# The convolution's channel norm placed behind the fifth half pair of w_out, and two sets of buffers for the latent attention

## The chip, the cores and the metric

One Trainium2 chip, of which the kernel uses 1 core. The metric is the time of one execution on the device in microseconds; the kernel before has a median of 2216.26 us over three runs. TensorE is called PE here, VectorE DVE, ScalarE ACT, GpSimd POOL and SyncE SP, as the profile calls them.

## What is computed

Two blocks in float32 on a sequence of 256 tokens of width 2048. The first has two layers, each a convolution branch and a window attention, joined by `w_out`; the second is one layer of RWKV-7 and latent attention (MLA) side by side, and a feed-forward network. Cut to what the change touches:

```python
def first_block(...):                       # for each of two layers
    u = rmsnorm(h) @ w_in
    a_val, a_glu, a_z, q, k, v, b_z = split(u)
    y  = conv31(a_val * sigmoid(a_glu)) + conv_b
    yc = y - mean(y, channels)              # the channel norm
    y  = yc * rsqrt(mean(yc * yc) + EPS) * cln_g + cln_b
    ya = silu(y) * silu(a_z)
    yb = window_attention(q, k, v) * silu(b_z)
    h  = h + concat([ya, yb]) @ w_out
    h  = h + rmsnorm(p @ w_pe) * sigmoid(h @ w_pg)
...
def mla_mixer(...):                         # 8 heads, taken in 4 pairs
    q = rms_norm(c_q) @ w_uq;  kv = rms_norm(c_kv) @ w_ukv
    s = q_nope . k_nope + rope(q_pe) . rope(k_pe)
    out = softmax(causal(s)) @ v
...
x = x + concat([y_rwkv, y_mla]) @ w_out_2
```

## The kernel before

All activations are kept transposed, channels on the partitions and the 256 tokens along the row. Every float32 product is made of three: weights and activations are split into a high and a low half (fp32r). SP loads 512 KB of weights at a time into `wraw`; ACT casts the high half (L285), DVE subtracts for the low half (L286), and PE multiplies. `wide` (L331) takes a pair of output tiles, with the high half against both halves of the activations (512 columns, L353) and the low half against the high one (256 columns, L355); `lin` (L308) and `mm3` (L1231 to L1233) make three matmuls of 256 columns. "Half pair" below is one such call of `wide` over eight of the sixteen row tiles of `w_out`: 32 matmuls.

The order of work inside each engine is fixed when the program is built: a scheduler places instructions by their priority, which is their place in the code (weights' splits and the RWKV work are put ahead by a fixed offset), and by its own model of when each can run. On the chip each engine then works its list in that order.

`layer1` (L512) of the first block: `w_in`'s column pairs, then four rounds of q projection, window attention and convolution. A convolution tile `cy` is 30 multiply-adds on DVE (L591). Then the channel norm: eight `cs` matmuls sum over channels, DVE subtracts the mean (L601), ACT squares (L603, L606), DVE adds up (L607, L224), `pc` sums over partitions on PE (L227), `rsqrt` (L207 to L214) is a chain of small DVE instructions, and `bcast` spreads the result over the partitions (`rbx` L246, `rbp` L249, `rl` L251). Then four z gates (`pz`), each followed by the product with `rl` (L616), Silu (L619), the product with z (L621) and the split into `Y` (L271, L272). Then eight half pairs of `w_out` on its attention rows (8 to 15), with `w_pe`'s products between them (`embed_part`: statistics on ACT, L404, evacuation, L749), and last eight half pairs on the convolution rows (0 to 7).

`mixers` (phase b) has one pair of buffers `mla_s` for the latent attention. `mla_pair` (L1257) makes the projections of two heads out of `cq` and `ck`, rotates (`pr` L1284, L1285 to L1287), makes scores (`msc`, L1314, L1315), softmax, transposes (`mtr` L1330) and products (`mo`, L1335 to L1337), and splits the result (`yp`) into `Ym`. The RWKV chunks, with a triangular inverse (`tri_inverse`: steps L1066 and L1067 on DVE, then two DMAs and a transpose to `Ttr`, L1072) for each of four groups, run beside it. At the end h is loaded back from DRAM (`hdr`, L835, two times 1 MB) and scaled (L837) into `h2`, and `load_y` (L839) brings the RWKV outputs from DRAM (`ydr`). Large buffers are slots of a pool of eight: `mla_s` and `Ym` take the four slots of the inputs `X2`, `Yr` those of the RWKV (`big`), `h2` those of `cq` and `ck`.

## Time and profile before

| | |
|---|---|
| median of three runs | 2216.26 us (2212.31 to 2216.68) |
| the profiled execution | 2216.77 us, span 2213.8 us |
| PE busy | 2168.2 us, 98% |
| DVE, ACT, POOL busy | 1711.1, 1207.7, 106.4 us |
| granted clock of TensorE, mean | 0.995 |
| chain that ended last | PE 91%, DVE 3%, DMA 2%, ACT 2% |

The span is what the profiler saw from the first to the last instruction; the rest of the execution, 2.97 us, lies around it. "Busy" of PE counts a matmul's modelled length. Idle time in front of a PE instruction, with the releaser that the trace names, is what a change of order can gain or lose. A clock below 1 means that matmuls ran on the lower of two levels for a part of the stretch.

### The profile page before, as it was taken

What the parts mean: (1) busy time and instruction counts of PE and PEld (TensorE: products, weight loads), DVE (VectorE), ACT (ScalarE), POOL (GpSimd) and SP (SyncE); (2) the same over time, 40 slices, a digit from 0 to 9 for tenths busy, and PEclk for the clock granted to TensorE, in tenths of its full rate; (3) what the DMA queues carried; (4) which work ended last, traced back from release to release, by engine and by line L of the source; (5) the groups of instructions that cost most, each with busy time, mean ns of one, the idle gap of its engine ahead of it and who ended that gap; (6) DMA issues with size and microseconds to landing.
All of it is one profiled execution on the core that took longest, in us unless ns stands there. A gap on an engine that the chain in (4) does not pass through costs nothing.

```text
span 2213.8 us, 36348 instructions
## 1 busy us (share of the span) xinstructions
PE 2168.2 (98%) x13687; PEld 1935.8 (87%) x13687; DVE 1711.1 (77%) x3176; ACT 1207.7 (55%) x1861; POOL 106.4 (5%) x253
## 2 busy tenths in 40 slices
PE   8999999999999999999999999999999999999997
PEld 7899988888899878899999888888888888888887
DVE  6999999778989889787787877776765576556765
ACT  6456636565566546665666556455443444444443
POOL 3100000000000000001100000020000000000000
PEclk9999999999999999999999999999999999999999
DMA  8875556666665457677774435476666666566654
GB/s 238 240 211 164 173 162 209 194 207 189 188 183 170 149 166 219 212 214 216 221 183 123 129 88 158 157 255 203 191 189 192 194 189 190 190 196 188 189 190 140
DMA packets 374511, 412.76 MB, mean 186 GB/s; under 512 B 40456, under 2 KB 327429, under 8 KB 373952
## 3 DMA queue, kind: packets, MB, share of 16 engines
q1 hardware_dynamic: 336464, 366.06, 54.4%
q0 software_dynamic: 10960, 31.79, 4.6%
q10 hardware_dynamic: 26912, 12.60, 2.4%
q8 instruction: 107, 1.75, 0.3%
q14 instruction: 68, 0.56, 0.1%
HBM read 390.47 MB, written 19.92 MB: 185 GB/s over the span
## 4 chain that ended last, share of the span: by engine, by line
PE 91%; DVE 3%; DMA 2%; ACT 2%; issue 1%; ACTq 1%; SPq 0%; DVEq 0%
PE wide L353 35%; PE wide L355 18%; PE lin L328 4%; PE lin L327 4%; PE lin L329 4%; PE lin L1401 3%; PE lin L1402 3%; PE lin L1400 3%; PE dn L1402 2%; PE dn L1401 2%; PE dn L1400 2%; PE po L709 1%; DVE wlo L286 1%; PE lin L1231 1%; PE lin L1232 1%; PE lin L1233 1%
## 5 line engine op out<-in xcount | busy, mean ns | idle before, releaser
L285 ACT CAST whi<-wraw 128x1024 fp32r<-128x1024 f32 (+1 forms) x708 | 725.2, 1027 | 670.6 <-PE wide L353 290.8
L286 DVE TENSOR_TENSOR wlo<-wraw,whi 128x1024 fp32r<-128x1024 f32 (+1 forms) x708 | 843.4, 1192 | 313.6 <-ACT whi L285 307.0
L353 PE MATMUL wide<-xs,whi 128*128 128x512 f32 x3492 | 853.0, 393 | 6.0 <-ACT whi L285 3.7
L353 PEld LDWEIGHTS wide<-xs,whi 128*128 128x128 f32 x3492 | 638.0, 189 | 129.8 <-ACT whi L285 5.3
L355 PEld LDWEIGHTS wide<-xs,wlo 128*128 128x128 f32 x3492 | 454.2, 191 | 25.8 <-DVE wlo L286 5.5
L355 PE MATMUL wide<-xs,wlo 128*128 128x256 f32 x3492 | 466.3, 284 | 3.6 <-DVE wlo L286 3.6
L327 PE MATMUL lin<-xs,whi 128*128 128x256 f32 x844 | 241.1, 286 | 1.2 <-ACT whi L285 0.6
L329 PE MATMUL lin<-xs,wlo 128*128 128x256 f32 x844 | 240.2, 285 | 1.6 <-DVE wlo L286 1.6
L328 PE MATMUL lin<-xs,whi 128*128 128x256 f32 x844 | 240.2, 285 | 0.0
L591 DVE SCALAR_TENSOR_TENSOR cy<-apad,vc_cw,cy 128x256 f32<-128x256 f32 x480 | 229.6, 480 | 6.7
L327 PEld LDWEIGHTS lin<-xs,whi 128*128 128x128 f32 x844 | 161.5, 191 | 2.7 <-ACT whi L285 0.8
L329 PEld LDWEIGHTS lin<-xs,wlo 128*128 128x128 f32 x844 | 161.5, 191 | 2.4 <-DVE wlo L286 1.8
L328 PEld LDWEIGHTS lin<-xs,whi 128*128 128x128 f32 x844 | 161.6, 191 | 1.1 <-issue 0.7
L1401 PE MATMUL lin<-wlo,xs 128*128 128x512 f32 (+1 forms) x304 | 117.4, 386 | 0.5 <-DVE wlo L286 0.5
L1402 PE MATMUL lin<-whi,xs 128*128 128x512 f32 (+1 forms) x304 | 117.0, 385 | 0.0
L1400 PE MATMUL lin<-whi,xs 128*128 128x512 f32 (+1 forms) x304 | 113.7, 386 | 1.2 <-ACT whi L285 1.2
L1400 PEld LDWEIGHTS lin<-whi,xs 128*128 128x128 f32 x304 | 57.1, 188 | 12.8 <-ACT whi L285 1.6
L1401 PEld LDWEIGHTS lin<-wlo,xs 128*128 128x128 f32 x304 | 57.2, 188 | 11.9 <-DVE wlo L286 1.0
L1400 PE MATMUL dn<-whi,xs 128*128 128x512 f32 (+1 forms) x176 | 67.0, 381 | 0.0
L1401 PE MATMUL dn<-wlo,xs 128*128 128x512 f32 (+1 forms) x176 | 67.0, 381 | 0.0
L1402 PE MATMUL dn<-whi,xs 128*128 128x512 f32 (+1 forms) x176 | 67.0, 381 | 0.0
L1402 PEld LDWEIGHTS lin<-whi,xs 128*128 128x128 f32 x304 | 57.1, 188 | 11.1
(544 smaller groups left out, 2401.1 us busy)
## 6 DMA issues: line engine op xcount, KB each, us to landing
wraw<-in_w_in_dram SPq DMA_DIRECT2D x244, 512.0 KB, 4.1
wraw<-in_w_out_dram SPq DMA_DIRECT2D x89, 512.0 KB, 4.0
wraw<-in_ffn_w_gate_dram SPq DMA_DIRECT2D x88, 512.0 KB, 4.1
wraw<-in_ffn_w_up_dram SPq DMA_DIRECT2D x88, 512.0 KB, 3.9
wraw<-in_ffn_w_down_dram SPq DMA_DIRECT2D x87, 512.0 KB, 4.3
wraw<-in_w_pg_dram SPq DMA_DIRECT2D x64, 512.0 KB, 4.5
bt<-btab POOLq DMA_DIRECT2D x32, 192.0 KB, 3.1
btab<-bF ACTq DMA_DIRECT2D x4, 1024.0 KB, 8.1
```

The lines of the kernel that those rows point to most:

```text
L285: nc.scalar.copy(hi[:], src)
L286: self.lo = nc.vector.tensor_tensor(lo[:], src, hi[:].bitcast(F32), ALU.subtract)
L327: nc.tensor.matmul(ps[:, t, :], lhsT=h, rhs=xh_, start=((t, k) == first), stop=False)
L328: nc.tensor.matmul(ps[:, t, :], lhsT=h, rhs=xl_, start=False, stop=False)
L329: nc.tensor.matmul(ps[:, t, :], lhsT=l, rhs=xh_, start=False, stop=((t, k) == last))
L353: nc.tensor.matmul(ps[t][:], lhsT=hi[:, i, ts], rhs=S.both(k).rearrange("p u c -> p (u c)"), **flags)
L355: nc.tensor.matmul(ps[t][:, :SEQ], lhsT=lo[:, i, ts], rhs=S.hi(k), **flags)
L591: prev, tail = tail, nc.vector.scalar_tensor_tensor(y, ap[:, t, k : k + SEQ], cw[:, k : k + 1], y, ALU.mult, ALU.add)
L709: nc.tensor.matmul(po[:, qb, g, :], lhsT=pT[:, kb, qb * 128 : qb * 128 + 128], rhs=vd[:, kb, j, :], start=(kb == 0), stop=(kb == 1))
L1400: nc.tensor.matmul(ps, lhsT=zh, rhs=hi, start=(k == 0), stop=False)
L1401: nc.tensor.matmul(ps, lhsT=zh, rhs=lo, start=False, stop=False)
L1402: nc.tensor.matmul(ps, lhsT=zl, rhs=hi, start=False, stop=(k == nt - 1))
```

## The change

In `layer1` the whole channel norm goes into a method of its own, `channel_norm`, which is called after the fifth of the eight half pairs on the attention rows (j == 4). The four z gates come first and are kept in `zs`; the products with `rl`, Silu, the product with z and the split follow after all eight half pairs. In the second block `mla_s` becomes two sets, taken in turn; a pair's output goes to DRAM (`mdr`) and is read back by `load_y`, which gets its target and source as arguments; `Ym` and `h2` are made after the attention. Slots: the two sets take the four of `X2`, `Ym` the `big` ones, `h2` those of `cq` and `ck` as before, `Yr` the first set's. `silu_pair` had no caller. Nothing in the diff changes the queue of the inverses' DMAs.

```diff
@@ layer1
-        ss = self.psum("o", [128, SEQ], "cs")
...
-        rl = self.bcast(self.rs_cols(acc, 1.0 / 1024, EPS, "rc")[:], "rl", pool=self.w1)
+        zs = []
         for j in range(4):
             pz = self.wide(w_in, 0, kall, 2048 + j * 256, S)
...
             nc.scalar.activation(zz[:], zz[:], AF.Silu)
+            zs.append(zz)
+
+        for j in range(8):
+            ps = self.wide(A["w_out"][i], 0, list(range(8, 16)), j * 256, Y)
+            hh = self.at(self.hT, 2 * j, 2)
+            self.add_wide(hh, ps)
+            if j % 2:
+                self.embed_part(i, j // 2, E)
+            if j == 4:
+                rl = self.channel_norm(cy)
+        for j in range(4):
             y = cy[:, 2 * j : 2 * j + 2, :]
             nc.vector.tensor_tensor(y, y, bc(rl[:], 2), ALU.mult)
...
-            nc.vector.tensor_tensor(y, y, zz[:], ALU.mult)
+            nc.vector.tensor_tensor(y, y, zs[j][:], ALU.mult)
             self.split_pair(Y, 2 * j, y)
-
-        for j in range(8):
-            ps = self.wide(A["w_out"][i], 0, list(range(8, 16)), j * 256, Y)
...
@@
+    def channel_norm(self, cy):
+
+        nc = self.nc
+        ss = self.psum("o", [128, SEQ], "cs")
+        for c in range(8):
+            nc.tensor.matmul(ss[:], lhsT=self.ones, rhs=cy[:, c, :], start=(c == 0), stop=(c == 7))
...
+        return self.bcast(self.rs_cols(acc, 1.0 / 1024, EPS, "rc")[:], "rl", pool=self.w1)
@@ mixers
-        self.mla_s = self.slot(F32, "mla"), self.slot(F32, "mla")
-        Ym = self.new_split(2)
+        self.mla_s = [(self.slot(F32, "mla"), self.slot(F32, "mla")) for _ in range(2)]
+        self.mdr = self.dr.tile([128, 8, SEQ], F32, name="mdr")
...
-            self.mla_pair(hp, cq, ck, Ym)
+            self.mla_pair(hp, cq, ck)
 
         wo = A["w_out_2"][0]
+        Ym = self.new_split(2)
+        h2 = [self.slot(F32, "h2") for _ in range(2)]
         Yr = self.new_split(2)
-        h2 = [self.slot(F32, "h2") for _ in range(2)]
...
-        def load_y(G):
+        def load_y(G, dst, src):
             yt = self.sqt()
-            nc.gpsimd.dma_start(yt[:], self.ydr[:, 2 * G : 2 * G + 2, :])
-            self.split_pair(Yr, 2 * G, yt[:])
+            nc.gpsimd.dma_start(yt[:], src[:, 2 * G : 2 * G + 2, :])
+            self.split_pair(dst, 2 * G, yt[:])
+        for G in range(4):
+            load_y(G, Ym, self.mdr)
         for G in range(3):
-            load_y(G)
+            load_y(G, Yr, self.ydr)
...
-        load_y(3)
+        load_y(3, Yr, self.ydr)
@@ mla_pair
-        s1, s2 = self.mla_s
+        s1, s2 = self.mla_s[hp % 2]
...
-        self.split_pair(Y, 2 * hp, yp)
+        nc.gpsimd.dma_start(self.mdr[:, 2 * hp : 2 * hp + 2, :], yp)
```

What this does to the lists of the engines is seen at three places. Line numbers of the new kernel are 8 lower in the attention of `layer1` and 3 higher in the latent attention.

PE in the first layer, kernel before, from the channel norm's `pc` on: `wide_3587` to `wide_3784` are half pairs 5 to 8 of `w_out`, `lin` is `w_pe`, `rbp` spreads the norm's result.

```order
L227 MATMUL pc_2858<-cblk,lnacc_2843 128x1 x2
L353 MATMUL wide_3587<-xs_1332,whi_3593 128x512 x4
L355 MATMUL wide_3587<-xs_1332,wlo_3594 128x256 x4
...
L249 MATMUL rbp_2880<-cblk,rbx_2878 128x128 x2
...
L353 MATMUL wide_3733<-xs_1332,whi_3739 128x512 x4
...
L353 MATMUL wide_3784<-xs_1333,whi_3809 128x512 x4
...
L353 MATMUL wide_3936<-xs_1330,whi_3941 128x512 x2
```

The same in the changed kernel; `wide_3759` is the last half pair on attention rows, `wide_3935` and `wide_3936` the first on convolution rows, which read the split norm `xs_1330`.

```order
L353 MATMUL wide_3759<-xs_1333,whi_3785 128x512 x4
L227 MATMUL pc_3586<-cblk,lnacc_3571 128x1 x2
L1234 MATMUL lin_3815<-pp_2340,whi_3811 128x256
...
L1236 MATMUL lin_3835<-pp_2340,wlo_3812 128x256
L227 MATMUL pc_3879<-cblk,acc_2343 128x1 x2
L249 MATMUL rbp_3608<-cblk,rbx_3606 128x128 x2
L249 MATMUL rbp_3901<-cblk,rbx_3899 128x128 x2
L189 MATMUL vps_4351<-cblk,vst_3906 128x124
L353 MATMUL wide_3935<-xs_1330,whi_3941 128x512 x2
L353 MATMUL wide_3936<-xs_1330,whi_3941 128x512 x2
```

Between `pc` and `rbp` stood half pair 5 and parts of 6 and 7, behind `rbp` whole half pairs; now 24 `lin` matmuls stand between them, and behind `rbp` the convolution rows follow almost at once.

POOL near the end of the latent attention, kernel before: `ga` and `ydr` belong to the RWKV groups, `h_2300` and `h_2301` are `h2`.

```order
L1166 DMA ga_14353<-in_rwkv_g_2_dram 128x256
L1167 DMA ga_14353<-in_rwkv_g_2_dram 64x256
L1174 DMA ydr<-sq_14134 128x512
L835 DMA h_2300_15104<-hdr 128x2048
L835 DMA h_2301_15105<-hdr 128x2048
L841 DMA sq_15132<-ydr 128x512
```

POOL in the changed kernel:

```order
L1177 DMA ydr<-sq_12750 128x512
L836 DMA h_2300_15101<-hdr 128x2048
L1342 DMA mdr<-mla_14364 128x512
L836 DMA h_2301_15102<-hdr 128x2048
L842 DMA sq_15123<-mdr 128x512
L1342 DMA mdr<-mla_14366 128x512
L842 DMA sq_15127<-mdr 128x512
L1169 DMA ga_14353<-in_rwkv_g_2_dram 128x256
```

The two loads of `h2` moved ahead of the last groups' work, to where `cq` and `ck` have just been used for the last time; writes and reads of `mdr` stand between.

DVE in the same stretch of the changed kernel: L1290 finishes the rope of a pair's queries, L1069 and L1070 are steps of the triangular inverse.

```order
L1289 TENSOR_TENSOR mla_14363<-mla_14363,rope 128x256
L1070 TENSOR_TENSOR T_13860<-T_13860,Tt_13861 128x6x10
L1321 TENSOR_SCALAR mst_14712<-mst_14712 128x2
L1144 TENSOR_TENSOR Y_14025<-po_14124,Y_14025 64x256
L1300 TENSOR_TENSOR mla_14365<-lin_14995,rkv_13361 128x512
L838 SCALAR_TENSOR_TENSOR h_2301_15102<-h_2301_15102,vc_a,rf 128x256 x8
L1290 TENSOR_TENSOR mla_14363<-mla_14363 128x256
L1069 TENSOR_TENSOR Tt_13861<-L_13851,T_13860 128x6x9
```

PE in the changed kernel, where it needs that rope: `lin_15021` is the last use of `ck`, `msc_14867` takes the rotated queries.

```order
L1236 MATMUL lin_15021<-whi_14991,ck_12790 128x256
L1317 MATMUL msc_14867<-mla_14363 128x128
L1318 MATMUL msc_14867<-rope,mla_14363 128x128
L1333 MATMUL mtr_14725<-cblk,mla_14366 128x128
L353 MATMUL wide_15151<-xs_15099,whi_15157 128x512 x2
L353 MATMUL wide_15201<-xs_15099,whi_15207 128x512 x2
```

In before the scalings of `h2` (L837) stand behind the softmaxes of the last pairs and all steps of the inverse; now the second eight stand ahead of a rope, of 18 instructions of the last inverse and of the first part of `Ym`.

## Rows read from the trace of the kernel before

**Rows 1.** The page, busy time, share of the span and instructions of each engine
```profile
PE 2168.2 (98%) x13687; PEld 1935.8 (87%) x13687; DVE 1711.1 (77%) x3176; ACT 1207.7 (55%) x1861; POOL 106.4 (5%) x253
```
**Rows 2.** Windows: stretch; length, busy PE, PEld, DVE, ACT, POOL; clock; DMA; GB/s
```profile
300.00:350.00 50.00, 44.68 (x258) 39.41 (x257) 44.35 (x90) 22.39 (x32) 2.37 (x6) 0.93 0.51 163
...
800.00:850.00 50.00, 44.24 (x264) 38.75 (x263) 44.19 (x86) 32.86 (x54) 3.80 (x7) 0.97 0.56 176
...
1180.00:1420.00 240.00, 230.86 (x1873) 206.21 (x1873) 185.72 (x539) 134.76 (x281) 12.22 (x25) 0.99 0.45 130
```
**Rows 3.** Windows, narrower, behind the two norms and in the latent attention
```profile
330.00:335.00 5.00, 2.34 (x13) 2.22 (x12) 3.51 (x6) 2.99 (x6) 0.56 (x1) 0.83 0.13 53
335.00:340.00 5.00, 4.08 (x15) 3.40 (x15) 3.46 (x6) 3.47 (x7) 0.30 (x1) 0.50 0.28 85
...
810.00:815.00 5.00, 2.34 (x16) 1.94 (x15) 3.71 (x8) 2.21 (x5) 0.08 (x1) 0.95 0.34 102
815.00:820.00 5.00, 4.01 (x17) 3.20 (x17) 2.88 (x4) 2.36 (x4) 0.47 (x1) 0.70 0.13 52
...
1260.00:1280.00 20.00, 16.93 (x147) 15.83 (x147) 14.61 (x49) 14.97 (x33) 0.54 (x1) 0.88 0.44 113
```
**Rows 4.** Waits of PE, 323 to 368 us: line, releaser; us, times, longest
```profile
PE lin L1231 <- ACT ev L749: 2.7, 1, 2.7
PE wide L355 <- DVE wlo L286: 1.0, 1, 1.0
```
**Rows 5.** Timeline of PE, first layer: start, length, instruction, count [idle before, releaser]
```profile
329.42 0.70 PE L597 MATMUL cs<-cy,cblk 128*128 128x256 f32 x2 [0.72 <-DVE cy L591]
...
351.11 1.08 PE L353 MATMUL wide<-xs,whi 128*128 128x512 f32 x4
...
361.35 0.28 PE L1231 MATMUL lin<-pp,whi 128*128 128x256 f32 x1
...
364.30 2.10 PE L353 MATMUL wide<-xs,whi 128*128 128x512 f32 x8
```
**Rows 6.** Timeline of DVE in the same stretch
```profile
330.16 2.48 DVE L601 SCALAR_TENSOR_TENSOR cy<-cs,cy 128x512 f32<-128x512 f32 x4 [0.79 <-PE cs L597]
...
339.85 0.16 DVE L207 TENSOR_SCALAR rs<-pc 128x2 f32<-128x2 f32 x1 [0.45 <-PE pc L227]
...
346.11 1.22 DVE L286 TENSOR_TENSOR wlo<-wraw,whi 128x1024 fp32r<-128x1024 f32 x1
347.25 0.28 DVE L246 COPY rbx<-rc 128x256 f32<-128x256 f32 x1
347.45 1.40 DVE L368 TENSOR_TENSOR hT<-hT,wide 128x256 f32<-128x256 f32 x4
...
350.53 0.69 DVE L409 TENSOR_TENSOR acc<-acc,sq 128x512 f32<-128x512 f32 x1 [0.54 <-ACT sq L404]
351.52 2.50 DVE L616 TENSOR_TENSOR cy<-cy,rl 128x512 f32<-128x512 f32 x4 [0.29 <-ACT rl L251]
...
363.48 1.89 DVE L272 TENSOR_TENSOR xs<-cy,xs 128x512 fp32r<-128x512 f32 x3
```
**Rows 7.** Timeline of ACT in the same stretch
```profile
354.45 4.07 ACT L619 ACTIVATE cy<-cy,vc_b,vc_a 128x256 f32<-128x256 f32 x8
```
**Rows 8.** Waits of PE, 1180 to 1420 us
```profile
PE mtr L1330 <- ACT mla L1326: 2.4, 2, 2.1
...
PE pz L1090 <- DVE Ttr L1072: 0.8, 1, 0.8
```
**Rows 9.** Loads of h2 by tile h; timelines of POOL and DVE there
```profile
DMA to landing us min/median/max: 8.8/9.9/11.1
...
1346.95 1.06 POOL L835 DMA_DIRECT2D h<-hdr  x2
...
1363.23 3.23 DVE L837 SCALAR_TENSOR_TENSOR h<-h,vc_a,rf 128x256 f32<-128x256 f32 x8
```
**Rows 10.** Timeline of DVE, last step of the third inverse and its transpose
```profile
1336.53 0.17 DVE L1067 TENSOR_TENSOR T<-T,Tt 128x8 f32<-128x8 f32 x1
...
1343.69 0.45 DVE L1072 STREAM_TRANSPOSE Ttr<-Tc 128x256 f32<-128x256 f32 x1 [2.26 <-DMA Tc<-td]
```

More of the change, by code (lines that the diff above doesn't have):

```diff
@@ L481, in bias_src @@
         return flat[127 : 127 + 128 * NREL].rearrange("(q c) -> q c", c=NREL)[:, :384]
-    def silu_pair(self, ps, r2, tag, bufs=2):
-        nc = self.nc
-        z = self.wk.tile([128, 2, SEQ], F32, tag=tag, bufs=bufs, name=self.nm("z"))
-        nc.vector.tensor_tensor(z[:], ps[:], r2, ALU.mult)
-        nc.scalar.activation(z[:], z[:], AF.Silu)
-        return z
     def value(self, pv, r2):
@@ L593, in layer1 @@
                         self.behind(tail, prev)
-        ss = self.psum("o", [128, SEQ], "cs")
-        for c in range(8):
-            nc.tensor.matmul(ss[:], lhsT=self.ones, rhs=cy[:, c, :], start=(c == 0), stop=(c == 7))
-        acc = self.wk.tile([128, 2, SEQ], F32, tag="acc", bufs=self.accb, name=self.nm("lnacc"))
-        for c in range(0, 8, 2):
-            y = cy[:, c : c + 2, :]
-            nc.vector.scalar_tensor_tensor(y, bc(ss[:], 2), -1.0 / 1024, y, ALU.mult, ALU.add)
-            if c == 0:
-                nc.scalar.activation(acc[:], y, AF.Square)
-            else:
-                sq = self.w1.tile([128, 2, SEQ], F32, tag="sq", name=self.nm("sq"))
-                nc.scalar.activation(sq[:], y, AF.Square)
-                nc.vector.tensor_tensor(acc[:], acc[:], sq[:], ALU.add)
-        rl = self.bcast(self.rs_cols(acc, 1.0 / 1024, EPS, "rc")[:], "rl", pool=self.w1)
+        zs = []
         for j in range(4):
@@ L665, in layer1 @@
         return N, st2
+    def channel_norm(self, cy):
[3 more added lines that the diff above has]
+            nc.tensor.matmul(ss[:], lhsT=self.ones, rhs=cy[:, c, :], start=(c == 0), stop=(c == 7))
+        acc = self.wk.tile([128, 2, SEQ], F32, tag="acc", bufs=self.accb, name=self.nm("lnacc"))
+        for c in range(0, 8, 2):
+            y = cy[:, c : c + 2, :]
+            nc.vector.scalar_tensor_tensor(y, bc(ss[:], 2), -1.0 / 1024, y, ALU.mult, ALU.add)
+            if c == 0:
+                nc.scalar.activation(acc[:], y, AF.Square)
+            else:
+                sq = self.w1.tile([128, 2, SEQ], F32, tag="sq", name=self.nm("sq"))
+                nc.scalar.activation(sq[:], y, AF.Square)
+                nc.vector.tensor_tensor(acc[:], acc[:], sq[:], ALU.add)
+        return self.bcast(self.rs_cols(acc, 1.0 / 1024, EPS, "rc")[:], "rl", pool=self.w1)
     def attend1(self, i, j, q, vd, gz, Y):
@@ L1255, in mla_tables, with mla_pair @@
             nc.vector.tensor_tensor(kz[hs, h, :], tk[hs, 0, :], tk[hs, 1, :], ALU.add)
-    def mla_pair(self, hp, cq, ck, Y):
+    def mla_pair(self, hp, cq, ck):
         nc, A = self.nc, self.A
```

4 lines of the change are left out of this document (removed).

## Prediction

> **What bounds the kernel now.** I read the page first: TensorE (PE) is busy 98% of the span [rows 1], so the time is the matmuls plus the little that PE stands still or runs on the slow clock. The reader is to see how little that is: about 45.6 us of 2213.8. Then the windows by stage, which say where those microseconds lie [rows 2]: 300 to 350 us lacks 5.3 us, 800 to 850 lacks 5.8, and 1180 to 1420, where the latent attention runs beside the RWKV chunks, lacks 9.1. The first two are the channel norm of the two layers and the third is the second part of the change. The narrower windows show the clock: it falls to 0.83 and 0.50 behind the first norm, 0.95 and 0.70 behind the second, and to 0.88 at 1260 to 1280 [rows 3]. Priced as lost share times length that is 0.8 + 2.5 + 0.3 + 1.5 = 5.1 us for the norms and 2.4 us for the attention. The waits of PE name the releasers: at the first norm 2.7 us for ScalarE's evacuation L749, which stands behind the squares, and 1.0 us for a low half of weights behind convolution taps [rows 4]; the 2.7 us stand in the second layer too. In the attention 2.4 us go to L1326 and 0.8 us to Ttr [rows 8].
>
> The whole prize is therefore 11.1 + 5.1 us for the norm and 9.1 + 2.4 us for the attention. The profiled execution took 2216.77 us (2.97 us outside its span), 0.5 us above the median of 2216.26; I work from 2216.77.
>
> **The channel norm.** It removes no arithmetic; it moves eight cs matmuls and all that follows from them. What counts is how much PE work stands between the last cs and the first conv-row matmul of w_out, which needs the finished norm. Before, the trace has 34.9 us between the two (329.42 to 364.30) [rows 5], all of it other matmuls but the waits named. In the changed order 64 wide matmuls (pairs 6 and 7) and 8 + 24 of w_pe remain. Price: 60 wide matmuls took 10.24 us (351.11 to 361.35), so 64 take 11; 24 w_pe matmuls took 2.95 us (361.35 to 364.30), so 32 take 3.9 [rows 5]; with the small ones about 15.5 us of cover.
>
> The chain it must cover, in the changed order: the pc matmul stands behind both pairs, so it starts 12.2 us after cs (8 x 0.123 + 11.2). VectorE is ready by then: 0.74 us to the first subtraction, 2.5 for four, three low halves at 1.14, four sums at 0.6 and five h additions at 0.35 come to 10.8 us [rows 6]. From pc on PE has 24 matmuls left, 3.4 us with the small ones. VectorE first finishes an h addition and a low half (1.5 to 2.4 us, taken as 2). Then the inverse root up to rbx: 7.7 us in before (339.85 to 347.53), and the new order has in that stretch three low halves, four sums and a dozen small ones, again 7 to 8; taken as 7.7. Transposing and copying rl takes 0.7 us at least. Then the tail that used to run under four more half pairs: first product 0.6, eight Silus 4.07 [rows 7], last product by z 0.6, cast and low half 1.2, together about 6.5 and taken as 7, where before it lasted 12.0 among other work (351.52 to 363.48) [rows 6]. The sum behind pc is 2 + 7.7 + 0.7 + 7 = 17.4 us against 3.4 us of matmuls: **PE stands 14 us** in the first layer. In the second the order behind pc is the same but for one pair of transposes less: 13 us. Bounds: if nothing stood between the small instructions (2 us for the root, 6.5 for the tail), 7.8 us a layer; if the tail and the copy kept their old lengths (12.0 and 4.0), 22. The old 11.1 us go, since pc, the squares and the evacuations now lie beside whole half pairs. Net: 27 - 11.1 = **+16 us**, bounds +4.5 and +33; I take the middle value because each of its terms has a row of the same instructions. The clock dips twice before and will dip twice after, so I leave 5.1 us on both sides. Z gates cost the same and are off this path; silu_pair is not called.
>
> **The latent attention.** The second pair of buffers lets a pair's projections run while the pair before is in its softmax, which is what L1326 and part of the lin waits are about [rows 8]. Four writes and four reads of 256 KB by way of DRAM join POOL's queue, at about 0.5 us of issue each; four splits stay. The price is elsewhere: h2 sits in the buffers of cq and ck. In the changed order POOL issues the second h load only when ck is free, behind the last lin matmul of the fourth pair, and VectorE has its eight scalings of that load ahead of L1290, which finishes the query rope of the third pair, and PE's next instruction but one needs that rope. Queued behind the same scalings are 18 instructions of the triangular inverse of the fourth group, the low half of Ym's first pair and Ttr, for which pz waits. In before nobody waits for the load: issued at 1346.95, scaled at 1360.
>
> The stall: the 1 MB load landed 8.8 to 11.1 us after issue; take 9.9; eight scalings 3.2; the rope 0.4, being of the size of an h addition [rows 6, 9]: 13.5 us in which PE has nothing, since its next two instructions are these. Then VectorE works through the 18 instructions at 0.17 [rows 10], two low halves at 1.14, four of the size of the sums at 0.6 [rows 6] and some sixteen small ones at 0.14: 3.1 + 2.3 + 2.4 + 2.2 = 10 us; and from the last step to the end of Ttr it is 7.4 us at the quickest case (1336.7 to 1344.1) [rows 10]. Of those 17.4 us some 33 matmuls of PE cover 4.5. PE idle: 13.5 + 17.4 - 4.5 = 26.4 us. If all of the old 9.1 us and the 2.4 of the clock go, net **+15 us**, which I take, since the buffers are what most of the old waits are for. Bounds: only the load is felt and all else goes, 12.4 - 11.5 = +1; nothing of the old goes, +26. The inverses' queue is unchanged: 0.
>
> A rule to weigh: the Trainium skill, DMA: Bandwidth & Descriptors, section Bandwidth, has 6.15 us for 1 MB into SBUF from the POOL queue; the rows here say 8.8 and 11.1. By the page the stall is 3.75 us shorter and the sum 2244.
>
> **Sum.** 2216.8 + 16 + 15 = **2248 us**.
>
> **Rivals.**
> First, the norm is covered after all (faster). Place: between the last cs and the conv rows. VectorE works off the rest before pc, so that the root is short and the tail starts while pairs 6 and 7 run. It decides at 15.5 us: if the whole chain is shorter, the 11.1 us and the 5.1 us of clock are gained. Alone, with the attention's prize half won (-6), that gives 2216.8 - 16.2 - 6 = 2195; range 2189 to 2207. For it: the old waits are real and lie just there. Against it: pc itself comes after 12.2 us.
> Second, the second set wins its prize and the load lands in time, because ck's last matmuls are reached earlier: -11.5, with the norm at +16: 2221 (2218 to 2230 with part of the stall). Against it: no matmul stands between the last use of ck and the waiting one.
> The Trainium skill, Trainium Kernel Development and Optimization, section Best Practices, advises double buffering to overlap transfers with compute; by that rule this rival would be the case. The trace supports it only for the 2.4 us at L1326.
> Third, the norm is covered and the attention stalls: 2216.8 - 16.2 + 15 = 2216, range 2207 to 2224.
> Fourth, neither part moves what ends last: 2217. Of the change's own words one part is empty, the queue.
>
> **How the numbers follow.** Below 0.2% (4.4 us) this kernel can't be told from no change. Forecast 0.47 (2230 to 2270, by the bounds of both terms taken together at less than their ends), second rival 0.17, first 0.17, third 0.10, fourth 0.06, above 2270 0.03. Faster by more than 0.2%, below 2212: all of the first and 0.03 of the third, 0.20. Within: 0.04 of the third, the fourth and a little of the second, 0.10. Slower: 0.70. The range leaves out the first rival and what is above 2270: 2207 to 2270.
>
> **What would show it.** Right, if PE stands some 7 us for rbp and again as long for the first conv-row matmul (released by xs, L272) in either layer, no longer for L749 and L285; if VectorE waits about 10 us for the second h load with PE idle at msc L1318, and pz waits for Ttr right behind. Slow clock should follow each stand. Wrong, if pc is followed by matmuls without a gap, if the h load is issued well ahead of the last lin of the attention, or if time is lost behind 1420 us, where I expect nothing (reads of Ym by way of DRAM coming late for its rows would be the place).

## The result, and the profile after

The changed kernel has a median of 2242.77 us over four runs (2241.48 to 2244.29) against 2215.79 us of the kernel before beside it: a ratio of 1.0125, 95% interval 1.0107 to 1.0143. It is slower by 1.25%. The profiled execution took 2243.68 us with a span of 2241.9 us, 28.1 us more than before. The page's line of busy times answers to [rows 1]:

```profile
PE 2175.5 (97%) x13687; PEld 1942.0 (87%) x13687; DVE 1714.4 (76%) x3176; ACT 1209.1 (54%) x1861; POOL 110.8 (5%) x261
```

PE executes the same 13687 instructions. Its busy time grew by 7.3 us while its mean granted clock fell from 0.995 to 0.986, so I count these as matmuls on the slower of the two clock levels; the span minus its busy time went from 45.6 to 66.4 us: 20.8 us more of standing. So the 28.1 us are 20.8 of standing and some 7.3 of clock.

Four marks in the two traces say where: the last write of the finished h to DRAM (`hdr`, end of the first block), the first score matmul of the latent attention (`msc`), the last write of x (`x<-h`, end of the second block's mixers), and the end of the span.

| stretch | before | after | difference |
|---|---|---|---|
| to the last `hdr` write (both norms) | 988.1 | 1000.9 | +12.8 |
| to the first `msc` | 1261.7 | 1274.8 | +13.1 in all |
| first `msc` to last `x<-h` | 209.0 | 224.6 | +15.6 |
| last `x<-h` to the end | 743.1 | 742.5 | -0.6 |

**The norm.** The windows behind the two norms, in the columns of [rows 2]:

```profile
350.00:400.00 50.00, 37.83 (x212) 33.15 (x211) 40.50 (x88) 25.88 (x42) 2.16 (x4) 0.83 0.50 155
...
850.00:900.00 50.00, 42.32 (x229) 37.09 (x230) 39.86 (x69) 24.16 (x34) 0.00 (x0) 0.87 0.49 151
```

Before, the hole lay at 300 to 350 and 800 to 850 us and was 5.3 and 5.8 us deep. Now PE lacks 12.2 us in the first and 7.7 in the second window alone. The waits of PE there, first layer (345 to 400 us) and second (800 to 900), answer to [rows 4]; the columns are line, releaser, then us, times and longest:

```profile
PE rbp L249 <- DVE rbx L246: 8.0, 2, 7.6
PE pc L227 <- DVE rc L214: 4.2, 1, 4.2
```
```profile
PE wide L353 <- DVE rs L213: 8.5, 1, 8.5
PE pc L227 <- DVE rc L214: 3.5, 1, 3.5
```

The two layers show the same hole under two names: some 4 us while VectorE works on the inverse root and on the sums of another normalisation, and some 8 us for the tail behind it. The timeline of PE in the first layer (start, length, instruction, and in brackets the idle time before it and the releaser) shows why the names differ:

```profile
352.10 0.50 PE L227 MATMUL pc<-cblk,lnacc 128*128 128x1 f32 x4
...
359.75 0.98 PE L227 MATMUL pc<-cblk,acc 128*128 128x1 f32 x4 [4.15 <-DVE rc L214]
361.18 0.69 PE L249 MATMUL rbp<-cblk,rbx 128*128 128x128 f32 x2 [0.45 <-DVE rbx L246]
369.44 0.69 PE L249 MATMUL rbp<-cblk,rbx 128*128 128x128 f32 x2 [7.57 <-DVE rbx L246]
369.92 0.41 PE L189 MATMUL vps<-cblk,vst 124*128 124x124 f32 x1
370.04 1.22 PE L353 MATMUL wide<-xs,whi 128*128 128x512 f32 x2
```

And VectorE beside it:

```profile
360.84 0.28 DVE L246 COPY rbx<-rc 128x256 f32<-128x256 f32 x1
...
362.31 2.50 DVE L605 TENSOR_TENSOR cy<-cy,rl 128x512 f32<-128x512 f32 x4
...
369.10 0.28 DVE L246 COPY rbx<-rc 128x256 f32<-128x256 f32 x1
369.30 1.89 DVE L272 TENSOR_TENSOR xs<-cy,xs 128x512 fp32r<-128x512 f32 x3
```

The `pc` at 359.75 and the `rbp` at 369.44 are not the norm's: they belong to `w_pe`'s own normalisation, which PE's list puts ahead of the convolution rows and whose VectorE steps stand between and behind the norm's. When that `rbp` is released at 369.4, the split of the norm's first tile (from 369.30, 0.7 us) is under way, and the first convolution row follows it at 370.04, so the tail of the norm sets the time under either name. From the start of the last `cs` (339.53) to the first convolution row (370.04) it is 30.5 us, in the second layer 32.8. Before it was 34.9 in [rows 5]; the chain is no longer than it was, but the matmuls that ran beside it are now ahead of it.

**The latent attention.** The stage from the first `msc` to the last `x<-h` in one window each, the kernel before and after it:

```profile
1261.70:1470.70 209.00, 198.30 (x1441) 172.63 (x1440) 166.30 (x421) 114.52 (x238) 10.80 (x20) 0.98 0.49 148
```
```profile
1274.80:1499.40 224.60, 205.00 (x1441) 176.96 (x1440) 165.89 (x421) 114.53 (x238) 15.69 (x30) 0.94 0.48 148
```

Both hold 1441 matmul instructions. Standing went from 10.7 to 19.6 us (+8.9) and busy time from 198.3 to 205.0 (+6.7, clock 0.98 to 0.94). The waits of PE at 1180 to 1430 us, which answer to [rows 8]:

```profile
PE msc L1318 <- DVE mla L1290: 4.8, 1, 4.8
PE mtr L1333 <- ACT mla L1329: 3.3, 2, 2.7
PE wide L353 <- ACT rv L1126: 2.5, 1, 2.5
```

The second set did not remove the wait of the transposes (`mtr`) for the softmax (2.4 us before, 3.3 now), and two new waits stand beside it. The first is that of the predicted place. POOL's timeline, then VectorE's and PE's:

```profile
1332.53 0.53 POOL L836 DMA_DIRECT2D h<-hdr  x1 [18.44 <-PE pch L1117]
1334.39 0.55 POOL L1342 DMA_DIRECT2D mdr<-mla  x1 [1.33 <-ACT mla L1341]
1335.13 0.53 POOL L836 DMA_DIRECT2D h<-hdr  x1 [0.20 <-issue]
1342.32 0.54 POOL L842 DMA_DIRECT2D sq<-mdr  x1 [6.65 <-DMA mdr<-mla]
```
```profile
1341.18 3.25 DVE L838 SCALAR_TENSOR_TENSOR h<-h,vc_a,rf 128x256 f32<-128x256 f32 x8 [1.84 <-DMA h<-hdr]
...
1346.46 3.25 DVE L838 SCALAR_TENSOR_TENSOR h<-h,vc_a,rf 128x256 f32<-128x256 f32 x8
1349.64 0.42 DVE L1290 TENSOR_TENSOR mla<-mla 128x256 f32<-128x256 f32 x1
```
```profile
1343.86 0.28 PE L1236 MATMUL lin<-whi,ck 128*128 128x256 f32 x1
1344.82 0.49 PE L1317 MATMUL msc<-mla 128*128 128x128 f32 x2 [0.69 <-DVE mla L1288]
1350.11 0.80 PE L1318 MATMUL msc<-rope,mla 128*128 128x128 f32 x2 [4.80 <-DVE mla L1290]
```

The last use of `ck` is at 1343.86, and both loads of h were issued by 1335.13. So neither can lie in the buffer of `ck`, though the part on the change gives that slot to the second. The last use of `cq` is at 1334.55, so the second load may lie there; the first was released by `pch` (L1117), which reads `big`, so it most likely lies in a slot of the RWKV. VectorE waited 1.84 us for the first load and not at all for the second. What PE stands for at 1350.11 is the scalings themselves, 3.25 us for each eight, which are queued ahead of the rope.

The 2.7 us of `mtr` come from the same queue. ScalarE's last softmax step waits there for a reciprocal (L1326):

```profile
1353.15 0.80 ACT L1329 ACTIVATE mla<-mla,mst 128x128 f32<-128x128 f32 x2 [3.77 <-DVE mst L1326]
```

The exponentials ended at 1348.9; the reciprocal ran at 1352.96, behind the second eight scalings (to 1349.7), the rope and two low halves of weights.

The second new wait is on ScalarE. Its timeline near the end of the stage:

```profile
1398.83 1.30 ACT L271 CAST xs<-sq 128x512 fp32r<-128x512 f32 x2 [3.89 <-DMA sq<-mdr]
...
1404.09 1.19 ACT L271 CAST xs<-sq 128x512 fp32r<-128x512 f32 x2 [3.18 <-DMA sq<-ydr]
1405.18 1.99 ACT L285 CAST whi<-wraw 128x1024 fp32r<-128x1024 f32 x2
```

ScalarE stands 3.89 and 3.18 us for tiles that come back from DRAM (the second, from `ydr`, is read in the kernel before too), and two casts of weights, which need nothing of these tiles, are queued behind them. PE's 2.5 us for `wide` end 0.3 us behind these casts, at 1407.50; the trace names one small copy (L1126) that stands between.

The rest is clock. After the stand that ends at 1350.11 the windows of ten microseconds show it at 0.61, 0.73 and 0.76:

```profile
1350.00:1360.00 10.00, 6.26 (x23) 4.93 (x23) 9.44 (x47) 3.27 (x11) 0.00 (x0) 0.61 0.33 106
1360.00:1370.00 10.00, 8.69 (x44) 5.38 (x46) 3.18 (x11) 6.66 (x21) 2.71 (x5) 0.73 0.41 98
1370.00:1380.00 10.00, 10.00 (x94) 8.94 (x91) 2.46 (x8) 3.06 (x10) 0.55 (x1) 0.76 0.15 55
```

### The profile page after: what moved, and what is told of

It is laid out like the page before. It is cut to its first block, busy times and chain, and to the rows that moved or that the text cites. A ratio compares the mean times of both kernels' runs of the same rounds, so it can differ in the third digit from the quotient of the medians.

```text
span 2241.9 us, 36370 instructions
## 1 busy us (share of the span) xinstructions
PE 2175.5 (97%) x13687; PEld 1942.0 (87%) x13687; DVE 1714.4 (76%) x3176; ACT 1209.1 (54%) x1861; POOL 110.8 (5%) x261
## 5 line engine op out<-in xcount | busy, mean ns | idle before, releaser
L1403 PEld LDWEIGHTS lin<-whi,xs 128*128 128x128 f32 x304 | 57.1, 188 | 12.2 <-ACT whi L285 1.1
L1405 PEld LDWEIGHTS lin<-whi,xs 128*128 128x128 f32 x304 | 57.2, 188 | 11.1
```

Of the source, the lines that this page charges most:

```text
L1403: nc.tensor.matmul(ps, lhsT=zh, rhs=hi, start=(k == 0), stop=False)
L1405: nc.tensor.matmul(ps, lhsT=zl, rhs=hi, start=False, stop=(k == nt - 1))
```

## Experiments

My theory behind the prediction: the norm costs what its chain (last `cs` to first convolution row, some 31 us) is longer than the matmuls left beside it, and the attention costs what the h scalings put ahead of a rope. The rivals: the DRAM way of the attention's outputs costs by itself; the clock, and not the standing, is what the change costs; or the two parts act on each other. All runs in one table. "norm" is the time of the last `hdr` write, "stage" the stretch from the first `msc` to the last `x<-h`, with what PE stood still in it and was busy, all in microseconds; these come from one profiled execution each, the ratio (to the kernel before, run beside each) from several. The kernel before had a median of 2212.8 to 2213.4 us beside the experiments and 2215.8 beside the changed kernel, so a comparison with the changed kernel goes by the ratios.

| kernel | median us | ratio and interval | norm | stage | stood | busy |
|---|---|---|---|---|---|---|
| before | 2215.8 | | 988.1 | 209.0 | 10.7 | 198.3 |
| changed | 2242.8 | 1.0125 [1.0107, 1.0143] | 1000.9 | 224.6 | 19.6 | 205.0 |
| e1, norm alone | 2226.5 | 1.0073 [1.0045, 1.0100] | 1001.6 | 208.3 | 9.8 | 198.5 |
| e4, norm alone, third half pair | 2235.8 | 1.0106 [1.0085, 1.0127] | 996.2 | 222.9 | 14.9 | 208.0 |
| e6, norm alone, last half pair | 2240.9 | 1.0125 [1.0110, 1.0140] | 1011.1 | 212.5 | 10.0 | 202.5 |
| e5, norm alone, long fill | 2234.1 | 1.0095 [1.0073, 1.0116] | 1005.3 | 217.1 | 10.3 | 206.8 |
| e9, norm alone, shorter fill | 2226.2 | 1.0059 [1.0042, 1.0076] | 997.2 | 213.7 | 9.6 | 204.2 |
| e2, attention alone | 2230.2 | 1.0069 [1.0052, 1.0087] | 988.8 | 222.6 | 15.5 | 207.1 |
| e3, changed, scalings late | 2234.7 | 1.0095 [1.0080, 1.0110] | 1001.5 | 217.5 | 15.5 | 202.0 |
| e8, attention alone, scalings late | 2220.8 | 1.0032 [1.0017, 1.0046] | 989.6 | 214.1 | 14.5 | 199.6 |
| e7, attention alone, one set | 2228.3 | 1.0063 [1.0046, 1.0080] | 987.8 | 225.9 | 18.5 | 207.4 |
| e10, one set, scalings late | 2228.5 | 1.0074 [1.0057, 1.0090] | 989.2 | 218.6 | 14.4 | 204.3 |
| e11, as e8, pair 4 not by DRAM | 2222.5 | 1.0043 [1.0026, 1.0060] | 989.4 | 215.9 | 15.0 | 200.9 |
| e12, as e8, pairs 3 and 4 not | 2221.1 | 1.0039 [1.0024, 1.0054] | 989.6 | 215.1 | 13.5 | 201.7 |

### Each part alone: e1 and e2

The first is the change without everything in `mixers` and `mla_pair`, the second the change without everything in `layer1`.

> The changed channel norm alone, with the latent attention of before. Theory A (each part has a loss of its own: in the changed trace the norm lengthened the two layers by 12.8 us, from the writes of h to DRAM, which end at 988.1 before and 1000.9 after): 2228 us, PE again idle some 12 us in each layer between the pc matmul and the first conv-row matmul, and the clock at its lower level for some 10 us behind each. Rival B (the loss arises only because the scheduler orders the whole program anew, so that the parts can't be told apart): the two layers lengthened by something clearly other than 12 us, the sum of both single parts not near 27 us.

> The changed latent attention alone, with the channel norm of before. Theory A: 2231 us, 15 to 16 us lost between the first scores and the last write of x, with PE waiting some 5 us behind the scalings of h2 and a stretch of slow clock after it. In this program's order the second eight scalings stand two dozen instructions later on VectorE, behind the first scores of the third pair's first head, but still ahead of the last steps of the inverse; if the place of the scalings is what costs, the loss may come out a few us smaller (10 to 16). Rival C (the way by DRAM costs: four writes, four reads, and POOL waiting for each write to land): again 15 to 16, with PE waiting for the splits of Ym (L272) rather than for the rope.

Measured 2226.5 and 2230.2 us, the ratios 1.0073 and 1.0069. Their sum, 1.42%, lies within the interval of both together (1.07 to 1.43%), so within the noise the parts add up, and neither needs the other. e1's layers end 13.5 us later than before's, as theory A said (12.8). e2's wait behind the scalings bears another name than the changed kernel's. PE's waits at 1180 to 1440 us, then VectorE:

```profile
PE msc L1317 <- DVE mst L1319: 4.6, 2, 4.2
```
```profile
1336.89 3.25 DVE L838 SCALAR_TENSOR_TENSOR h<-h,vc_a,rf 128x256 f32<-128x256 f32 x8
```

L1319 takes the row maxima of the scores. It stands right behind these eight scalings and runs at 1340.18; PE goes on at 1340.52. For the split outputs (L272), of which rival C spoke, PE waits 0.8 us. e1's stage, whose source is that of before, shows before's times again:

```profile
1274.20:1482.50 208.30, 198.46 (x1441) 172.69 (x1440) 166.23 (x421) 114.67 (x238) 10.83 (x21) 0.98 0.46 149
```

### Where the norm is called: e4 and e6

```diff
-            if j == 4:
+            if j == 2:
                 rl = self.channel_norm(cy)
```

> The norm alone as in the first run of this set, but called behind the third half pair rather than the fifth. In this order 18.6 and 20.3 us of matmuls stand between the last cs and the first conv-row matmul (16.1 and 19.7 with the fifth), and of them 3.6 us behind rbp rather than 0.5 or less. Theory A (the uncovered chain is the loss): PE waits some 5 us at pc, since VectorE needs about 11 us from cs to there and PE has 5.4, and some 4 to 5 at the conv rows: 8 to 11 us a layer, 2 to 4 less than with the fifth; 2222 to 2226. Rival D (the loss is not the cover but ScalarE's tail, Silus held up by the two loads of e that stand ahead of them): no change against the first run, 2228.

e6 has `j == 7` there, behind all attention rows.

> The norm alone, called behind the last of the eight half pairs; the order of the second block is that of the kernel before. Only 0.9 us of matmuls are left behind pc, 12.3 us behind cs. Theory A as the prediction had it (the chain behind pc takes 17.4 us whatever stands before it): PE stands 17 us a layer, 2234 to 2238. Theory A'' (three low halves and four sums of other work are what makes the root long; with the call last they are done before it, and the order has 2.0 us between the root's start and rbx): some 4 us at pc and 9 behind it, 13 a layer, as with the fifth: 2226 to 2230.

The prediction's sum is chain minus cover. The chain is read in each trace (start of the last `cs` to the first convolution row), the cover is counted out of PE's list (the matmuls between the two, 0.23 us for 512 columns, 0.12 for 256, as the timelines have them); both layers:

| norm called | chain us | cover us | chain less cover, beyond before's 15.3 | last `hdr` write, beyond before's |
|---|---|---|---|---|
| before | 34.9, 35.2 | 27.4, 27.4 | | |
| third half pair (e4) | 30.1, 31.6 | 18.6, 20.3 | +7.5 | +8.1 |
| fifth (e1) | 30.7, 32.5 | 16.1, 19.7 | +12.1 | +13.5 |
| last (e6) | 32.9, 32.8 | 12.3, 12.2 | +25.9 | +23.0 |

Chain less cover is by its making what PE stands and loses to the clock between the two, so that the last two columns agree says little by itself. What the table shows is that the chain stays at 30 to 33 us wherever it is put, so that the cost follows the cover. Rival D, ScalarE's tail held up by a load, is small: in the first layer of e1 the issue of a load of `e` at 364.94 stands ahead of the first Silu, which comes 1.6 us behind its input, in the second layer nothing does, and e4's norm did gain 5.4 us over e1's. With the shortest cover e6 shows a wait one step earlier as well, in both layers alike; PE's waits there, 320 to 400 us:

```profile
PE pc L227 <- DVE lnacc L224: 9.8, 1, 9.8
PE rbp L249 <- DVE rbx L246: 7.7, 2, 6.2
```

That is 17.5 us of standing in the first layer, the 17 of theory A; the 13 of A'' did not come. This part of the theory stands. But e6's total is 3 us above A's range, and e4's total was missed by more: for the 5.4 us gained at the norm it lost 14.6 in the attention stage, whose source is untouched. There PE stood 14.9 us instead of 9.8, and the scheduler had built another order: counted in the traces by line, tile and shape, 1843 of 2100 PE instructions from just ahead of that stage on still stood in the sequence of before. In e6 the order there was that of before (2099), in e1 nearly so (2087), and PE stood 10.0 and 9.8 us.

### Work in the hole: e5 and e9

Dummy matmuls, whose sums nobody reads, fill the two waits of the norm, so that PE does not stand; what was lost to the clock should come back. e9 has 14 in place of 22 (21 in the last line becomes 13).

```diff
+        dm = self.psum("sc", [128, 2 * SEQ], "dm")
+        for k in range(30):
+            nc.tensor.matmul(dm[:, 0:SEQ], lhsT=Y.hi(8)[:, 0:128], rhs=Y.hi(8), start=(k == 0), stop=(k == 29))
+        for k in range(22):
+            nc.tensor.matmul(dm[:, SEQ:], lhsT=self.ones, rhs=rl[:], start=(k == 0), stop=(k == 21))
         for j in range(4):
             y = cy[:, 2 * j : 2 * j + 2, :]
```

> The norm alone, called behind the fifth half pair as in the first run, with matmuls added whose result nobody reads: 30 of 256 columns in front of rbp and 22 that need rl behind it, in each layer, put where PE stands still. They do no useful work and only keep PE busy. Theory A' (besides the stand itself the slow clock behind it costs, some 4 to 5 us a layer): the clock stays at its higher level, 2226 falls to 2217 to 2222. Rival F (the clock costs little, since what runs slowly lies in the shadow of the chain): 2226 or a few us more, for the added matmuls.

> As the run with added matmuls, but with 14 instead of 22 of those behind rbp: each took two passes of 0.25 us there, so that 22 lasted 11.2 us in a gap of 8 and held the conv rows up by 3.4 us in the first layer and by as much in the second. 14 last 7.1 us and fit. Theory A' (the slow clock behind the stand costs): the first 12 wide matmuls of the conv rows take 2.8 rather than 5.2 to 5.5 us, nothing is held up, and the last write of h to DRAM comes 3 to 6 us earlier than 1001.6; 2220 to 2224. Rival F (the clock costs little): at 1001 to 1003 and 2226 to 2228.

e5's fill of 11.2 us behind `rl` was too long: the first layer's convolution rows begin 3.4 us later than e1's. e9's fits. PE's timeline of e9, first layer:

```profile
361.91 9.03 PE L607 MATMUL dm<-rl,cblk 128*128 128x256 f32 x28 [0.46 <-ACT rl L251]
370.59 1.74 PE L353 MATMUL wide<-xs,whi 128*128 128x512 f32 x6
```

Six convolution matmuls in 1.74 us are 0.29 each; behind the stand of the changed kernel two took 1.22, 0.61 each. So the clock behind the stand is worth something, and the norm ends at 997.2 in place of e1's 1001.6 us (about 1.6 of that lies ahead of the first norm), as theory A' said. At the total nothing shows, as F said: 2226.2 against 2226.5. In the profiled executions the difference lies in the stage that none of the three kernels changes. e1's row is above; here e5's, then e9's:

```profile
1278.80:1495.90 217.10, 206.79 (x1441) 179.44 (x1440) 166.82 (x421) 114.97 (x238) 10.83 (x21) 0.94 0.45 143
```
```profile
1270.50:1484.20 213.70, 204.15 (x1441) 176.97 (x1440) 166.51 (x421) 114.65 (x238) 10.80 (x20) 0.95 0.46 145
```

With the same 1441 matmuls and nearly the same standing (9.8, 10.3, 9.6 us) PE was busy 198.5, 206.8 and 204.2 us. Counted as above, any two of the three have 1430 of their some 1440 PE instructions there in the same sequence. So up to eight microseconds of clock differ there with the source the same and the order nearly so; the last section shows as much between executions of one kernel. What the fill is worth in all is left open.

### The scalings of h: e3 and e8

The 16 scalings are ordered behind the last reciprocal of the last softmax, in the changed kernel (e3) and with the attention's part alone (e8):

```diff
-            self.mla_pair(hp, cq, ck)
+            end = self.mla_pair(hp, cq, ck)
...
-                nc.vector.scalar_tensor_tensor(h2[u][:, k, :], h2[u][:, k, :], self.fg[:, 8 * u + k : 8 * u + k + 1], rf[:],
+                sc = nc.vector.scalar_tensor_tensor(h2[u][:, k, :], h2[u][:, k, :], self.fg[:, 8 * u + k : 8 * u + k + 1], rf[:],
                                                ALU.mult, ALU.mult)
+                self.behind(sc, end)
...
-            nc.vector.reciprocal(st[:, 2:4], st[:, 2:4])
+            end = nc.vector.reciprocal(st[:, 2:4], st[:, 2:4])
...
+        return end
```

> The changed kernel, with all sixteen scalings of h2 ordered on VectorE behind the last softmax's reciprocals; loads, sets and the way by DRAM are as in the changed kernel. Theory A (the scalings ahead of the rope cost): the 4.8 + 0.7 us of PE at msc are gone, the inverse of the last group is some 6 us earlier and the clock's dip at 1350 to 1380 us shrinks: 2228 to 2235, so 8 to 15 us under the changed kernel. Rival C (the way by DRAM costs): within 3 us of the changed kernel's 2243.

> The changed latent attention with two sets, the norm of before, and the sixteen scalings of h2 ordered behind the last softmax's reciprocals, as in the third run but without the moved norm. Theory A as the prediction had it (the scalings are the whole loss): the stage takes about 209 us, 2213 to 2217. Theory G (the scalings are half of it; two sets draw the projections forward, so that the softmaxes of the last pairs and the last inverse stand at the end without matmuls beside them, and the clock falls): as in the third run, where the stage took 217.5: 215 to 219 us, 2220 to 2224.

By the ratios e3 lies 0.30% under the changed kernel (6.6 us; the two intervals overlap by 0.03%) and e8 0.37% under e2 (9.4 us by the medians, the intervals apart). The waits behind the scalings, for the rope in the changed kernel and for L1319 in e2, are gone in both. So with two sets the scalings' place is the larger part of the attention's loss, 9.4 of 17.2 us by e2 and e8. In the profiled stages 4.1 us of it are standing and 3.0 clock from the changed kernel to e3, but 1.0 standing and 7.5 clock from e2 to e8, so how much of it is the stall itself and how much the clock behind it is not settled. e8's total lies in theory G's range; G's reason, softmaxes at the end without matmuls beside them, is not what the waits name. What remains, 0.32%, has other names. e8's waits of PE at 1180 to 1430 us:

```profile
PE wide L355 <- ACT xs L271: 3.3, 1, 3.3
PE wide L353 <- DVE xs L272: 3.0, 1, 3.0
```

They are the attention's outputs on their way back. POOL's timeline in e8, and ScalarE's:

```profile
1366.46 0.55 POOL L1343 DMA_DIRECT2D mdr<-mla  x1 [9.69 <-ACT mla L1342]
1369.68 0.54 POOL L843 DMA_DIRECT2D sq<-mdr  x1 [2.67 <-DMA mdr<-mla]
```
```profile
1375.09 0.62 ACT L271 CAST xs<-sq 128x512 fp32r<-128x512 f32 x1 [5.70 <-DMA sq<-mdr]
```

From the write's issue to the first cast of what is read back it is 8.6 us (1366.46 to 1375.09); the kernel before casts straight out of the buffer.

### One set of buffers, the DRAM way kept: e7 and e10

```diff
-        self.mla_s = [(self.slot(F32, "mla"), self.slot(F32, "mla")) for _ in range(2)]
+        self.mla_s = [(self.slot(F32, "mla"), self.slot(F32, "mla"))]
...
-        s1, s2 = self.mla_s[hp % 2]
+        s1, s2 = self.mla_s[0]
```

Everything else of the attention's part stays; e10 has the late scalings too.

> The changed latent attention with one set of buffers instead of two, the norm of before; outputs go by way of DRAM as in the change. The h loads take the two free buffers and come early. Theory A (the sets and the place of h2's scalings are what costs, the way by DRAM is hidden): the stage from the first scores to the last write of x takes 207 to 213 us as before (209.1), 2211 to 2217. Rival C (the way by DRAM costs): 214 us or more in that stage, above 2219.

> One set of buffers, outputs by way of DRAM, the norm of before, and the scalings of h2 ordered behind the last softmax's reciprocals. It differs from the one-set run in the place of the scalings alone, and from the late two-set run (2220.8) in the sets alone. Theory H (the place of the scalings costs in both, the rest is the wait for Ym's reads from DRAM, L271 and L272, 6 us with two sets): 2216 to 2222, PE waiting 3 to 7 us for xs. Theory G (the two sets' early projections cost): 2211 to 2216. Rival C (the way by DRAM is the whole loss): 2225 or more, as with the scalings early.

e7 gave 2228.3 us: a loss of this size is there without a second set. It comes with what e7 keeps, the DRAM way, the slots that it moves and the order that the scheduler builds from them, and these three are not separated. The scalings are not it: in e7 they run at 1265.9 to 1274.2, at the start of the stage, ahead of no late rope, and e10, which orders them late, gains nothing (2228.5). So theories G and H, which forecast 2222 or less, fell. C's total came, but the waits for `xs` in e10 are 1.2 us; the longest is one step on, for weights whose casts stand behind the casts of tiles from DRAM (here the RWKV outputs, which the kernel before reads too). PE, then ScalarE:

```profile
1386.71 2.08 PE L353 MATMUL wide<-xs,whi 128*128 128x512 f32 x4 [2.40 <-ACT whi L285]
```
```profile
1382.20 0.62 ACT L271 CAST xs<-sq 128x512 fp32r<-128x512 f32 x1 [2.34 <-DMA sq<-ydr]
```

e8, with two sets and the scalings late, gave 2220.8. At that place of the scalings the second set thus goes with 7.7 us less, though in the profiled stages (14.4 and 14.5 us of standing) the difference is clock, not waits, so what brings it is open. With the scalings early, as in the change, it goes with no gain: e2 took 2230.2 us, e7 2228.3. The Trainium skill, Trainium Kernel Development and Optimization, section Best Practices, advises double buffering. One of these two pairs of runs agrees, and there the way that makes room for it costs more than it gives: e8 is still slower than the kernel before, which has one set.

### Less of the DRAM way: e11 and e12

```diff
-            end = self.mla_pair(hp, cq, ck)
+            if hp == 3:
+                Ym = self.new_split(2)
+            end = self.mla_pair(hp, cq, ck, Ym if hp >= 3 else None)
...
-        for G in range(4):
+        for G in range(3):
             load_y(G, Ym, self.mdr)
...
-        nc.gpsimd.dma_start(self.mdr[:, 2 * hp : 2 * hp + 2, :], yp)
+        if Y is not None:
+            self.split_pair(Y, 2 * hp, yp)
+        else:
+            nc.gpsimd.dma_start(self.mdr[:, 2 * hp : 2 * hp + 2, :], yp)
```

e12 has 2 in place of the 3s. Since `Ym` now takes its slots earlier, more than the way of the outputs changes: both loads of h are issued at 1353 us in e11 and 1349 in e12, in e8 at 1320 and 1323.

> The kernel before with the latent attention's part of the change alone, scalings of h behind the last softmax (as e8), and here the last pair's output split straight into Ym instead of written to DRAM and read back; pairs 0 to 2 still go by way of DRAM. Theory (the round trip of the last pair is what is left of e8's loss: there PE waited 3.3 us for the high and 3.0 us for the low half of outputs read from DRAM): those waits go, the stage falls from e8's 214 us to 207 to 210, total 2213 to 2217. Rival (the reads of the earlier pairs and of the RWKV outputs, which ACT and POOL take in order, hold the splits whichever pair comes last): waits for xs stay at 4 us or more, total 2219 to 2223.

> As e11, with the last two pairs split straight into Ym. Theory of the last pair's round trip: like e11, 2213 to 2217, nothing more to gain. Rival (reads taken in order): every read fewer takes some of the wait away, so this lies 1.5 us or more below e11. A third case, that two sets without a DRAM way at the end beat the kernel before, would show as 2209 or less.

The waits for `xs` went as the theory of the round trip said, from 6.3 us to 1.1 in e11 and to none in e12, and the time did not follow: 2222.5 and 2221.1 us, both like e8. Another wait has come in, of 5.2 us in both. e12's longest wait of PE, and ScalarE's timeline where it ends:

```profile
PE mtr L1335 <- ACT mla L1331: 5.2, 1, 5.2
```
```profile
1338.33 1.30 ACTq L1074 DMA_DIRECT2D td<-T  x2
1339.68 1.49 ACT L1331 ACTIVATE mla<-mla,mst 128x128 f32<-128x128 f32 x4 [1.40 <-DVE Y L1159]
```

The softmax's last scalings, for which the transposes wait, begin at 1339.68. The profile puts ScalarE's wait to VectorE's L1159, and ahead of them in ScalarE's own queue stand the issues of the inverse's transfers, until 1339.63. PE's next instruction needs these scalings, so it stood. The clock is 0.71 in the next ten microseconds, where before it was 1.00:

```profile
1340.00:1350.00 10.00, 9.87 (x74) 7.43 (x75) 2.09 (x5) 6.56 (x19) 2.31 (x6) 0.71 0.26 66
```

So the theory that the last pair's way through DRAM is what remains of e8's loss has fallen: it is one wait among several of a like size, and with it gone the scheduler built an order with another. Every order of this stage but that of before stood 13.5 to 19.6 us instead of 9.6 to 10.7. Which property of before's order does it I have not isolated. No kernel tried here beats the kernel before.

## Why the prediction was right, and where it was not

The forecast was 2248 us, within 2207 to 2270, slower with a chance of 0.7; it came to 2242.8. So the total and its direction are right. Of the two terms, one is right by its mechanism and the other only by its sum.

**The norm, +16 forecast, +12.8 measured.** The mechanism is that of the sum: the cover behind the last `cs` is too short. PE was forecast to stand 14 and 13 us; it stood 12.2 (4.15 + 0.45 + 7.57) and 12.0 (3.50 + 8.48). The old 11.1 us went, and 24.2 less 11.1 is 13.1. In the first layer `pc` came at 352.1, 12.6 us behind the start of the last `cs` where the forecast has 12.2, and the first convolution row 17.9 us behind that, where the forecast has 17.4, so the chain was right within some half a microsecond each. The term that was mis-sized by 2 us is the cover behind `pc`: forecast at 3.4 us, it was 5.8, since the other normalisation's `pc` (0.98 us) and two `rbp` (0.69 each) ran there on the slow clock. The signs named were 7 us for `rbp` and 7 more for the convolution row; they came as 4.2 and 8, the first as a wait of the other normalisation's `pc`, which stands between. The list of PE showed that `pc`, and the forecast gave it no wait.

**The clock of the norm, assumed equal, cost about the same.** It was low for longer, 0.57 and 0.66 at 355 to 375 and 845 to 865 us against 0.83 and 0.91 at 325 to 345 and 810 to 830 before, but for most of that time PE stood. Of the 7.3 us by which PE's busy time grew 6.7 are in the attention's stage; the norms have at most 0.6 of it. (The 5.1 us of the old clock were priced over whole windows, in which PE also stood, so they are an upper bound; the sum has them on both sides.)

**The attention, +15 forecast, +15.6 measured, by a wrong sum.** The place was right: PE idle at `msc` L1318, behind L1290, behind the second eight scalings. The size was not. The step that failed is the issue of the second h load: I put it behind the last use of `ck`, 9.9 us of landing included, and it was issued 8.7 us before that use, since it does not lie in that buffer. The load was covered but for 1.84 us of VectorE's time, and the stall was 0.69 + 4.80 = 5.5 us instead of 13.5. The chain of the inverse behind it, forecast at 17.4 less 4.5 us of matmuls, did not come as a wait for Ttr at all; PE stood 5.0 us between 1350 and 1370, for the softmax above all (2.7, of which the scalings are a part, and 1.1), and ran on the slow clock for much of the rest. And two losses were not in the sum: the waits for the DRAM reads (2.5 us on PE), and the clock, which I let give back 2.4 us and which took 6.7. Forecast were 26.4 us of standing less 9.1 and 2.4; measured were 8.9 us more of standing and 6.7 more of clock. That the two sums agree is luck. The clock's part is no chance of one execution, for the four of the changed kernel lie within 2.8 us of each other.

**The old waits there.** I let all 9.1 us go, as waits for the buffers. The wait at the softmax's transposes stayed (2.4 before, 3.3 now), and the stage's other order brought waits of its own; e11 and e12 show how easily.

**Nothing behind 1420 us** was right as a place (the last stretch is 0.6 us shorter), but the reads of `Ym` that I had looked for there bit earlier, at 1398 to 1407.

**The rivals.** The first and third, a covered norm, fell with the result, and e4 to e6 confirm it: even behind the third half pair the chain is 11 us longer than its cover in each layer, where before it was 7.5 and 7.8. The second, the load in time and the prize won, was half right: the loads came in time, and the prize did not come with them, e8 being the case with no stall at the rope and still 0.32% slower. The fourth, no effect, fell with the total. The rule on the bandwidth of POOL's queue (the Trainium skill, DMA: Bandwidth & Descriptors, section Bandwidth) decides nothing here, since the load is covered; the first load was ready 8.65 us behind its issue (1332.53 to 1341.18), nearer to the rows of before than to the Trainium skill's 6.15. That figure is by the Trainium skill's own note there the time in which the DMA engines are busy, and the forecast's 2244 took it for the time from issue to landing.

## What to carry to other kernels

Price a serial chain by its length less the matmuls that the order leaves beside it, counted from PE's list; moving it later in the program did not shorten it here, and it cost as much as the cover shrank. A buffer that is bought by a way through DRAM can cost time in the engines that work in order: here a cast that waited for a read held the casts queued behind it. Taking such waits out does not have to bring the time back, as e11 and e12 show. A load's follow-up work (here scalings that nobody needs yet) is best put behind what others wait for. Where a scheduler sets the order, a change in one stage can reorder another that it doesn't touch, so each stage's standing is to be read before a total is explained.

## What was not expected of the hardware

The same program's clock differs from one execution to the next. e5's four executions took 2230.5, 2232.0, 2236.2 and 2239.8 us at mean granted clocks of 0.996, 0.994, 0.993 and 0.991, e9's four 2223.0 to 2231.4 at 0.996 to 0.991: some 8 to 9 us within 0.005 of clock. One profiled stage therefore carries several microseconds of chance, and the busy column of the table is to be read so; the column of standing is steadier (9.6 to 10.7 us in all five kernels with before's order or nearly that).

A read that waits for a 256 KB write on POOL's queue waited 2.4 to 2.7 us behind the later writes of the changed kernel, and 6.65 us behind the one issued between the two loads of 1 MB. Those loads need not be the reason: in e7, with no load of h near, two of the four waits were 4.60 and 5.74 us. Why is open.
